# Attention step of a gated hybrid encoder: the mask and maximum of a block behind the turned copy, the variance's square a step ahead, and missing fill steps spread over the heads

## The chip, the cores and the metric

The kernel runs on one core of a Trainium2 chip. The metric is device time in microseconds (us) of the whole program, as the median of several runs. A profile is one more execution, recorded instruction by instruction. Engines: PE (TensorE, matrix products), DVE (VectorE), ACT (ScalarE), POOL (GpSimd), SP (which issues the transfers). Each works through its own instructions in order.

## The reference, cut to what matters

One layer of an encoder with two branches on the same normalised input (1024 frames of a prompt and 32 frames of a running stream, width 1024, 16 heads of 64).

```python
s = einsum('bqhd,bkhd->bhqk', q, k) + (cq - ck)      # logits with forget-gate bias
s = where(qpos >= kpos, s, lowest)                   # causal
p = softmax(s); o = einsum('bhqk,bkhd->bqhd', p, v)
conv = depthwise_conv(u_ext, w_dw) + b_dw            # 31 taps, per channel
ya = (o * silu(ga)) @ w_pa
yb = (silu(layernorm(conv)) * silu(gb)) @ w_pb       # mean and variance over 1024 channels
y  = x + (sigmoid(ma) * ya + sigmoid(mb) * yb) @ w_out
```

## The kernel before, in words

The program has three stages. First come the projections of the input for queries, keys, values, the convolution and the gate `ga`; then the attention, in which the projections of the gates `gb`, `ma` and `mb` are filled in between; then the output projections.

**The attention stage** goes over a list `seq` of 132 items: for each of 16 heads eight blocks of 128 queries (`Block`, with `i` from 0 to 7, whose keys are the first `128 * (i + 1)`), and four `Sample` items for the running stream, one after the first block of heads 3, 7, 11 and 15. In this text h2.4 is block 4 of head 2. An item passes through these methods:

- `scores` (L1110): two or four products of PE into a score tile `psS` of two banks; two such tiles rotate. In the kernel before its end also puts the causal mask on the diagonal block (L1124, DVE) and takes the negated row maximum (L1126, DVE, over all keys of the block).
- `soft` (L1129): the exponential with the maximum as bias, on ACT (L1133), into `P`.
- `norm` (L1136): the reciprocal of the row sum on DVE (L1138) and the scaling of `P` on POOL (L1139).
- `turn` (L1141): `i + 1` transposes on PE (L1153) into tiles `psT`, four to a tile, two tiles rotating. The first tile is copied out by ACT and, in blocks 4 to 7, the second by DVE (both L1156). The change's "turned copy" is this copy on DVE.
- `values` (L1158): in block 7, forty products with the values (L1172), two copies out by ACT (L1176) and DVE (L1177) and, for odd heads, the multiplication by `ga` (L1179).

The loop over `seq` (L1244) runs a software pipeline. At item `n` it calls `scores` of `n + 3`, then loads, `turn` of `n`, `soft` of `n + 3`, `norm` of `n + 2`, some fill steps, `values` of `n - 2`, as many fill steps again, and one step of the layer norm once the convolution's sums are there.

**A fill step** (`fill`, L1023) advances the generator of the gate projections by one step: three products of 352 columns (L183) and a `beat`. In all 528 such steps are to be had (22 column groups of 24 steps). They write two PSUM banks in turn, and ACT evacuates each group of eight steps (L944). Each `beat` also moves a clock that releases other work: the convolution taps on DVE (L371, one about every five beats until they are done), the loads of the next weights, their square on ACT (L117) to find a scale, and their split into a high half on ACT (L138, `wh`) and a low half on DVE (L141, `wl`).

**The layer norm's statistics** (`layernorm`, L1206) are a generator too. Its first four steps do nothing. Three steps make the mean (a product with a matrix of ones, L1202, and a scaling on ACT), three the variance, and twelve the reciprocal root. A variance step (`put`, L1213) issues the product on PE, then the square of the mean on ACT (L1215), then three DVE operations (L1216 to L1218), the first of which needs both.

**What sets the order.** In this stage the orders of PE, SP, DVE and ACT are the program's own, as the loop writes them. Only POOL's order is chosen by a scheduler. The number of fill steps around an item is written out at L1258:

```python
some = 2 if isinstance(b, Sample) or b.i > 2 or b.head.h != 8 else 0
fill(some)
...
fill(some)
```

So every item has four fill steps, and h8.0, h8.1 and h8.2 have none; with twelve steps ahead of the loop these make 528.

Of the kernel before, what the change touches and what calls it, by code (L numbers as in the profile page):

```python
# [8 lines left out]
F32 = mybir.dt.float32  # L9
# [5 lines left out]
ALU = mybir.AluOpType  # L15
AX = mybir.AxisListType

D = 1024
T = 1024
# [6 lines left out]
CH = 352  # L26
# [27 lines left out]
def build(tc, xT, xt, wv, wf, ckT, cv, clT, stT, vec, cst, yT, kT, vO, lfO, cpT, csT):  # L54
    nc = tc.nc
# [3 lines left out]
    def pool(name, bufs=1, stack=es, **kw):  # L59
        return stack.enter_context(tc.tile_pool(name=name, bufs=bufs, reuse_waits="tile", **kw))  # L60
# [19 lines left out]
    rstd = lnp.tile([128, TT], F32, name="rstd")  # L80
# [105 lines left out]
    def csl(c):  # L186
        return slice(c * CH, (c + 1) * CH)
# [88 lines left out]
    def t352(name, bufs):  # L276
        return sg.tile([128, CH], F32, name=name, tag=name, bufs=bufs)
# [5 lines left out]
    class Banks:  # L283

        n = 0
# [451 lines left out]
    for c in range(4):  # L737
# [264 lines left out]
    psT = pool("psT", 2, stack=p2, space=PS)  # L1002
# [4 lines left out]
    class Two:  # L1007
        n = 0
# [14 lines left out]
    def fill(n):  # L1023
        for _ in range(n):
            next(flow, None)

    class Sample:
# [15 lines left out]
        def scores(self):  # L1043
            g, kc, pf = self.g, self.kc, self.pf
            ps = psS.tile([128, 2, 512], F32, name="psS", tag="S")
            for j in range(4):
                rows = slice(64 * (j % 2), 64 * (j % 2) + 64)
                q = qs_t[rows, 2 * g + j // 2, :]
                nc.tensor.matmul(ps[32 * j:32 * j + 32, 0, :], q, kc[rows, j // 2, :], start=True, stop=True)
                nc.tensor.matmul(ps[32 * j:32 * j + 32, 1, :TS], q, ks_t[rows, 2 * g + j // 2, :],  # L1050
                                 start=True, stop=True)
            nc.vector.scalar_tensor_tensor(pf[:, :PAST], ps[:, 0, :], cq[:, g:g + 1], pf[:, :PAST],
                                           op0=ALU.add, op1=ALU.subtract)
# [50 lines left out]
    class Block:  # L1104
# [5 lines left out]
        def scores(self):  # L1110
            i = self.i
            QA, QB, KA, KB = self.head.q
            nk = (i + 1) * 128
            qsl = slice(i * 128, i * 128 + 128)
            ps = psS.tile([128, 2, 512], F32, name="psS", tag="S")
            nb = 1 if nk <= 512 else 2
            w = nk // nb
            wm = max(w, 256)
            for b in range(nb):
                ksl = slice(b * w, b * w + wm)  # L1120
                nc.tensor.matmul(ps[:, b, :wm], QB[:, qsl], KB[:, ksl], start=True, stop=False)  # L1121
                nc.tensor.matmul(ps[:, b, :wm], QA[:, qsl], KA[:, ksl], start=False, stop=True)  # L1122
            diag = ps[:, nb - 1, w - 128:w]
            nc.vector.tensor_add(diag, diag, cmask)  # L1124
            nm = ap.tile([128, 3], F32, name="nm", tag="nm", bufs=6)
            nc.vector.tensor_reduce(nm[:, 0:1], ps[:, :nb, :w], axis=AX.XY, op=ALU.max, negate=True)  # L1126
            self.at = ps, nm, nk, nb, w
# [55 lines left out]
    seq = []  # L1183
# [5 lines left out]
    def start(b):  # L1189
        if getattr(b, "i", 1) == 0:  # L1190
            h = b.head
            if h.h % 2 == 0:
                h.ot = heads[h.h + 1].ot = ap.tile([128, T], F32, name="ot", tag="ot", bufs=2)
        b.scores()

    def pending(b):
        return isinstance(b, Sample) or b.i % 2

    def over_channels(acc, put):
        for c in range(3):  # L1200
            pm = psT.tile([128, 512], F32, name="psn", tag="T")
            nc.tensor.matmul(pm[:, :CH], ones_f, acc[:, csl(c)], start=True, stop=True)  # L1202
            put(csl(c), pm[:, :CH])
            yield

    def layernorm():  # L1206

        shift = sides["shift"]
        for _ in range(4):
            yield  # L1210
        yield from over_channels(mean, lambda sl, ps: nc.scalar.mul(mean[:, sl], ps, 1.0 / D))

        def put(sl, ps):  # L1213
            t = t352("t", 3)
            nc.scalar.activation(t, mean[:, sl], AF.Square)  # L1215
            nc.vector.scalar_tensor_tensor(rstd[:, sl], ps, 1.0 / D, t, op0=ALU.mult, op1=ALU.subtract)  # L1216
            nc.vector.tensor_add(mean[:, sl], mean[:, sl], shift[:, sl])
            nc.vector.tensor_scalar(rstd[:, sl], rstd[:, sl], EPS, None, op0=ALU.add)  # L1218

        yield from over_channels(rstd, put)  # L1220
        for c in range(6):
            sl = slice(c * CH // 2, c * CH // 2 + CH // 2)
            v, y = rstd[:, sl], t352("t", 3)[:, :CH // 2]
            nc.scalar.activation(y, v, AF.Ln)
            nc.scalar.activation(y, y, AF.Exp, scale=-0.5)
            yield
            w = t352("t", 3)[:, :CH // 2]
            nc.vector.tensor_copy(w, v)
            newton(v, w, y)
            yield  # L1230

    ones_f = cp.tile([128, 128], F32, name="ones_f", tag="ob")
    nc.vector.memset(ones_f, 1.0)
    ln = layernorm()
    sides["shift"] = ap.tile([128, TT], F32, name="shift", bufs=1)
    nc.sync.dma_start(sides["shift"], s_m)
    heads[1].load()
    for n in range(3):
        start(seq[n])
        seq[n].soft()  # L1240
        if n:
            seq[n - 1].norm()
        fill((8, 4, 0)[n])
    for n, b in enumerate(seq):  # L1244
        if n + 3 < len(seq):
            start(seq[n + 3])
        if n + 9 < len(seq) and getattr(seq[n + 9], "i", 1) == 0:
            seq[n + 9].head.load()
        if n + 6 < len(seq) and isinstance(seq[n + 6], Sample):
            seq[n + 6].load()  # L1250
        if getattr(b, "i", 0) == 3 and b.head.h + 1 < H:
            heads[b.head.h + 1].load_v()
        b.turn()
        if n + 3 < len(seq):
            seq[n + 3].soft()
        if n + 2 < len(seq):
            seq[n + 2].norm()
        some = 2 if isinstance(b, Sample) or b.i > 2 or b.head.h != 8 else 0  # L1258
        fill(some)
        if n >= 2 and pending(seq[n - 2]):  # L1260
            seq[n - 2].values()
        fill(some)
        if n >= 3 and isinstance(seq[n - 3], Sample):
            seq[n - 3].finish()
        if "ready" in sides:
            next(ln, None)
# [17 lines left out]
    class Banks3:  # L1284
        n = 0
# [383 lines left out]
```

## Time and profile before

| | |
|---|---|
| median of 3 runs | 1348.63 us (1346.65 to 1349.82) |
| the profiled execution | 1345.89 us, of it 1344.1 us span from first to last instruction |
| attention stage in the profile | about 566 to 1053 us |
| mean granted PE clock | 0.996 |

The timeline's times are counted from the span's start. "Idle before" is the time in which an engine had nothing to run, and the name behind an arrow is what released it. Matrix products overlap one another, so their lengths may add up to more than the time they take.

### The profile page before, as it was taken

The page shows a single profiled execution, that of the slowest core. Times are in us where ns is not written, and L with a number is a line of the kernel's source. Part 1 is how long each engine was busy: PE and PEld are TensorE (multiplying, and loading weights), DVE is VectorE, ACT ScalarE, POOL GpSimd, SP SyncE. Part 2 cuts the span into 40 slices and gives each one's busy share as a digit, 9 for nine tenths or more (in the row PEclk, how much of TensorE's full clock was granted, in tenths as well). Part 3 has the DMA queues.
Part 4 walks back from the last instruction along what each step waited for, and adds up shares of the span by engine and source line. Part 5 has one row for each costly group of instructions (what it writes and reads, how often), then busy time and mean ns, then how long its engine had stood idle before and what let it go on. Part 6 is the DMA issues. An engine that isn't in the chain of part 4 may idle for free.

```text
span 1344.1 us, 24837 instructions
## 1 busy us (share of the span) xinstructions
PE 1312.6 (98%) x9383; PEld 1003.1 (75%) x9383; DVE 990.4 (74%) x1532; ACT 719.0 (53%) x1362; POOL 505.8 (38%) x548
## 2 busy tenths in 40 slices
PE   8999999999999999999889998999999999999999
PEld 5687876666666666667567766777776699999998
DVE  6797879888999997987778866655554489166664
ACT  6644555757676743455555555655555566233320
POOL 2001124547484820243433442222222158255562
PEclk8999999999999999999999999999999999999999
DMA  6343233425352463535644643565452698544462
GB/s 251 98 140 104 93 112 118 139 82 187 95 180 87 162 166 109 160 90 155 165 109 123 186 132 99 147 179 132 131 152 54 240 313 262 176 128 146 142 190 69
DMA packets 113496, 194.97 MB, mean 145 GB/s; under 512 B 34080, under 2 KB 80032, under 8 KB 113376
## 3 DMA queue, kind: packets, MB, share of 16 engines
q1 hardware_dynamic: 113232, 193.31, 46.9%
q8 instruction: 74, 1.21, 0.4%
q14 instruction: 46, 0.38, 0.1%
q10 hardware_dynamic: 144, 0.07, 0.0%
HBM read 127.68 MB, written 65.64 MB: 144 GB/s over the span
## 4 chain that ended last, share of the span: by engine, by line
PE 82%; DVE 9%; ACT 3%; issue 2%; DMA 2%; SPq 1%; POOL 0%; DVEq 0%; ACTq 0%; POOLq 0%
PE pj L183 56%; PE pjv L761 6%; PE pj L1501 6%; PE po L1172 4%; PE ptr L1153 3%; DVE nm L1126 2%; DVE wl L141 2%; DVE y L371 2%; PE psS L1122 2%; PE psS L1121 2%; DMA ga<-s_ga 2%; ACT wh L138 1%; DVE psS L1124 1%; DMA s_q<-qh 1%; PE warm L477 1%
## 5 line engine op out<-in xcount | busy, mean ns | idle before, releaser
L183 PE MATMUL pj<-xh,wh 128*128 128x352 f16 (+2 forms) x1536 | 481.6, 314 | 2.3 <-ACT wh L138 1.4
L183 PE MATMUL pj<-xh,wl 128*128 128x352 f16 (+2 forms) x1536 | 481.2, 313 | 0.7 <-DVE wl L141 0.6
L183 PE MATMUL pj<-xl,wh 128*128 128x352 f16 (+2 forms) x1536 | 480.9, 313 | 0.5 <-DVE xl L579 0.4
L183 PEld LDWEIGHTS <-wh 128*128 128x128 f16 x3072 | 301.5, 98 | 162.1 <-issue 7.1
L371 DVE SCALAR_TENSOR_TENSOR y<-u,vec_t,y 128x1086 f32<-128x1086 f32 x240 | 346.8, 1446 | 12.0 <-ACT y L368 8.9
L1139 POOL TENSOR_SCALAR P<-P,nm 128x128 f32<-128x128 f32 (+7 forms) x128 | 129.9, 1015 | 279.9 <-DVE nm L1138 229.8
L183 PEld LDWEIGHTS <-wl 128*128 128x128 f16 x1536 | 150.5, 98 | 72.0 <-DVE wl L141 1.6
L141 DVE SCALAR_TENSOR_TENSOR wl<-raw,sc,wh 128x384 f16<-128x384 f32 (+1 forms) x192 | 128.2, 693 | 48.3 <-ACT wh L138 48.3
L1133 ACT ACTIVATE P<-psS,nm 128x128 f32<-128x128 f32 (+7 forms) x128 | 95.1, 743 | 113.3 <-DVE nm L1138 70.9
L1126 DVE TENSOR_REDUCE nm<-psS 128x1 f32<-128x128 f32 (+7 forms) x128 | 97.0, 758 | 12.5
L1153 PE MATMUL ptr<-ident,P 128*128 128x128 f32 x576 | 88.6, 276 | 17.3 <-DVE pt L1156 9.2
L175 POOL TENSOR_TENSOR wl<-raw,wh 128x384 fp32r<-128x384 f32 (+1 forms) x51 | 63.3, 1270 | 74.3 <-ACT wh L172 58.6
L1153 PEld LDWEIGHTS ptr<-ident,P 128*128 128x128 f32 x576 | 69.2, 141 | 28.2 <-DVE pt L1156 12.1
L1156 ACT COPY pt<-ptr 128x512 f32<-128x512 f32 (+3 forms) x128 | 64.3, 502 | 44.4 <-PE ptr L1153 43.2
L1121 PE MATMUL psS<-KB,QB 128*128 128x256 f32 (+2 forms) x192 | 81.8, 427 | 0.6 <-ACT P L1133 0.6
L880 POOL TENSOR_TENSOR sql<-sqf,sqh 128x352 fp32r<-128x352 f32 x48 | 57.0, 1187 | 65.8 <-ACT sqh L877 65.8
L138 ACT ACTIVATE wh<-raw,sc 128x1024 f16<-128x1024 f32 (+1 forms) x68 | 73.9, 1091 | 8.2 <-DVE sc L158 7.9
L1172 PE MATMUL po<-pt,V 128*64 128x256 f32 x640 | 72.8, 382 | 2.5 <-ACT pts L1078 1.7
L1124 DVE TENSOR_TENSOR psS<-psS,cmask 128x128 f32<-128x128 f32 x128 | 37.6, 294 | 46.0 <-PE psS L1122 45.6
L906 POOL TENSOR_TENSOR ql<-qn,qh 128x352 fp32r<-128x352 f32 (+1 forms) x48 | 67.8, 1429 | 6.6 <-ACT qh L905 6.5
L761 PE MATMUL pjv<-vwh,xh 128*128 128x260 f16 x256 | 70.1, 274 | 0.0
L761 PE MATMUL pjv<-vwl,xh 128*128 128x260 f16 x256 | 70.0, 273 | 0.0
(271 smaller groups left out, 2532.9 us busy)
## 6 DMA issues: line engine op xcount, KB each, us to landing
raw<-wf SPq DMA_DIRECT2D x92, 512.0 KB
QB<-s_q SPq DMA_DIRECT2D x32, 256.0 KB
KB<-s_k SPq DMA_DIRECT2D x32, 256.0 KB
kT<-qn SPq DMA_DIRECT2D x8, 528.0 KB
s_ga<-t SPq DMA_DIRECT2D x24, 176.0 KB
s_gb<-t SPq DMA_DIRECT2D x24, 176.0 KB
s_ma<-t SPq DMA_DIRECT2D x24, 176.0 KB
s_mb<-t SPq DMA_DIRECT2D x24, 176.0 KB
```

The lines of the kernel that those rows point to most:

```text
L138: nc.scalar.mul(wh[:, ks, :], raw[:, ks, :], self.s[:, i:i + 1])
L141: nc.vector.scalar_tensor_tensor(wl[:, ks, :], raw[:, ks, :], self.s[:, i:i + 1], wh[:, ks, :], op0=ALU.mult, op1=ALU.subtract)
L183: nc.tensor.matmul(ps, a[:, kt, :], b(kt, sl), start=(first and n == 0), stop=(last and n == N - 1))
L371: t = nc.vector.scalar_tensor_tensor(y, u[:, i:i + CW], w, y, op0=ALU.mult, op1=ALU.add)
L761: nc.tensor.matmul(ps[:, :VC], a, b, start=(n == 0), stop=(n == 23))
L1121: nc.tensor.matmul(ps[:, b, :wm], QB[:, qsl], KB[:, ksl], start=True, stop=False)
L1126: nc.vector.tensor_reduce(nm[:, 0:1], ps[:, :nb, :w], axis=AX.XY, op=ALU.max, negate=True)
L1133: nc.scalar.activation(P[:, :nk].rearrange("p (b w) -> p b w", b=nb), ps[:, :nb, :w], AF.Exp, bias=nm[:, 0:1], accum_out=nm[:, 1:2])
L1139: nc.gpsimd.tensor_scalar(P[:, :nk], P[:, :nk], nm[:, 2:3], 1.0, op0=ALU.mult, op1=ALU.mult)
L1153: nc.tensor.transpose(pt[:, 128 * j:128 * j + 128], P[:, 128 * (4 * u + j):128 * (4 * u + j) + 128], ident)
L1172: nc.tensor.matmul(po[rows], V[:, j, :], parts[c][:, j, :], start=(c % 2 == 0 and j < 2), stop=(c % 2 == 1 and j >= 2 * c))
L1501: nc.tensor.matmul(pss[c][:, :HC], a[:, k, :], x, start=(not more and kt == 0 and n == 0), stop=(kt == 3 and n == 2), skip_group_check=more)
```

## The change

It has three parts.

1. The mask and the maximum leave `scores` and become a method `top` of `Block` and of `Sample`. The loop calls it after `turn` and just ahead of `soft`. On DVE the copy of block `n` now stands before mask and maximum of item `n + 3`; before it stood behind them. PE's order stays.
2. In the layer norm's variance steps the square on ACT is issued one step ahead of the product and the DVE operations that use it.
3. Head 8's three items get their four fill steps back. In heads 2 to 13 the second group of block 6 has one step instead of two. The sum is again 528.

```diff
             self.ps = ps                      # Sample
+        def top(self):
+            g, ps, pf = self.g, self.ps, self.pf
             nc.vector.scalar_tensor_tensor(pf[:, :PAST], ps[:, 0, :], ...)
...
             self.at = ps, nk, nb, w           # Block
+        def top(self):
+            ps, nk, nb, w = self.at
             diag = ps[:, nb - 1, w - 128:w]
             nc.vector.tensor_add(diag, diag, cmask)
...
-        def put(sl, ps):
+        for c in range(3):
+            sl = csl(c)
             t = t352("t", 3)
             nc.scalar.activation(t, mean[:, sl], AF.Square)
-            nc.vector.scalar_tensor_tensor(rstd[:, sl], ps, 1.0 / D, t, op0=ALU.mult, op1=ALU.subtract)
+            yield
+            pm = psT.tile([128, 512], F32, name="psn", tag="T")
+            nc.tensor.matmul(pm[:, :CH], ones_f, rstd[:, sl], start=True, stop=True)
+            nc.vector.scalar_tensor_tensor(rstd[:, sl], pm[:, :CH], 1.0 / D, t, op0=ALU.mult, op1=ALU.subtract)
             nc.vector.tensor_add(mean[:, sl], mean[:, sl], shift[:, sl])
             nc.vector.tensor_scalar(rstd[:, sl], rstd[:, sl], EPS, None, op0=ALU.add)
-
-        yield from over_channels(rstd, put)
...
         b.turn()
         if n + 3 < len(seq):
+            seq[n + 3].top()
             seq[n + 3].soft()
         if n + 2 < len(seq):
             seq[n + 2].norm()
-        some = 2 if isinstance(b, Sample) or b.i > 2 or b.head.h != 8 else 0
-        fill(some)
+        fill(2)
         if n >= 2 and pending(seq[n - 2]):
             seq[n - 2].values()
-        fill(some)
+        fill(1 if getattr(b, "i", 0) == 6 and 2 <= b.head.h < 14 else 2)
```

The first three items, ahead of the loop, call `top` right after `scores`, so their order is unchanged. The generator of the layer norm has as many steps as before; each variance product comes one step later, and the last of them in the same step as the first logarithm of the reciprocal root.

More of the change, by code (lines that the diff above doesn't have):

```diff
@@ L1051, in scores @@
                                  start=True, stop=True)
+            self.ps = ps
+        def top(self):
+            g, ps, pf = self.g, self.ps, self.pf
             nc.vector.scalar_tensor_tensor(pf[:, :PAST], ps[:, 0, :], cq[:, g:g + 1], pf[:, :PAST],
@@ L1122, in scores @@
                 nc.tensor.matmul(ps[:, b, :wm], QA[:, qsl], KA[:, ksl], start=False, stop=True)
+            self.at = ps, nk, nb, w
+        def top(self):
+            ps, nk, nb, w = self.at
             diag = ps[:, nb - 1, w - 128:w]
@@ L1239, in build @@
         start(seq[n])
+        seq[n].top()
         seq[n].soft()
```

## The prediction

> **What bounds the kernel now.** The first view is the page: which engine is busy.
>
> ```profile
> PE 1312.6 (98%) x9383; PEld 1003.1 (75%) x9383; DVE 990.4 (74%) x1532; ACT 719.0 (53%) x1362; POOL 505.8 (38%) x548
> ```
>
> TensorE (PE) is busy for all but 31.5 us of the span of 1344.1 us. The change adds and removes hardly any work, so it can win only PE's idle time, and only in the attention stage, where its lines run. The second view sums engines by stretch: attention runs from 566 to 1053 us, and I cut out 816 to 836.
>
> ```profile
> 566.00:816.00 250.00, 235.96 (x1741) 170.37 (x1739) 190.30 (x370) 140.87 (x304) 96.74 (x113) 1.00 0.49 135
> 816.00:836.00 20.00, 15.78 (x93) 10.59 (x94) 11.20 (x24) 8.72 (x18) 3.17 (x7) 0.91 0.41 104
> 836.00:1053.00 217.00, 214.13 (x1628) 155.61 (x1627) 122.67 (x305) 125.26 (x274) 54.63 (x97) 1.00 0.46 128
> ```
>
> After the stretch and its length stand the busy times of PE, weight load, DVE, ACT and POOL, then PE's clock. PE idles 14.0, 4.2 and 2.9 us: 21.1 us in all, a fifth of it in the 20 us of head 8, and there the clock falls to 0.91. The groups by line say what ends this idle time (last columns).
>
> ```profile
> L1153 PE MATMUL ptr<-ident,P 128*128 128x128 f32 x576 | 88.6, 276 | 17.3 <-DVE pt L1156 9.2 <-ACT pt L1156 6.4 <-DVE ot L1177 1.2
> L1172 PE MATMUL po<-pt,V 128*64 128x256 f32 x640 | 72.8, 382 | 2.5 <-ACT pts L1078 1.7 <-ACT mean L1211 0.7
> ```
>
> So 17.3 of 21.1 us stand in front of the transposes, which wait until one of the two psT tiles has been copied out: 9.2 us for the DVE copy, 6.4 us for the ACT copy. The DVE copy exists only in blocks 4 to 7 of a head. I write h2.4 for head 2, block 4.
>
> **Part 1: mask and maximum behind the copy, gain.** Here is a DVE that runs late (h2.4, the maximum is that of h2.7), from the timeline: start, length, engine, line, and in brackets the idle time before and its releaser.
>
> ```profile
> 648.02 0.29 DVE L1124 TENSOR_TENSOR psS<-psS,cmask 128x128 f32<-128x128 f32 x1
> 648.41 1.22 DVE L1126 TENSOR_REDUCE nm<-psS 128x1 f32<-128x1024 f32 x1
> 649.55 0.28 DVE L1156 COPY pt<-ptr 128x128 f32<-128x128 f32 x1
> 649.75 1.12 ACT L1133 ACTIVATE P<-psS,nm 128x1024 f32<-128x1024 f32 x1 [1.79 <-DVE nm L1126]
> 649.89 0.44 PE L1153 MATMUL ptr<-ident,P 128*128 128x128 f32 x2 [1.16 <-DVE pt L1156]
> ```
>
> The copy starts 1.53 us after the mask. Put first, it starts at 648.02 and PE's 1.16 us are gone. The price is that the exponential of the new block starts later by the copy's 0.28 us. No instruction and no DMA is added: scores, mask, maximum and copy are the same ones. The other waits of this kind:
>
> ```profile
> 592.04 0.55 PE L1153 MATMUL ptr<-ident,P 128*128 128x128 f32 x3 [1.74 <-DVE pt L1156]
> 595.82 0.66 PE L1153 MATMUL ptr<-ident,P 128*128 128x128 f32 x4 [0.65 <-DVE pt L1156]
> 684.78 0.44 PE L1153 MATMUL ptr<-ident,P 128*128 128x128 f32 x2 [0.61 <-DVE pt L1156]
> 688.18 0.55 PE L1153 MATMUL ptr<-ident,P 128*128 128x128 f32 x3 [0.49 <-DVE pt L1156]
> 692.57 0.66 PE L1153 MATMUL ptr<-ident,P 128*128 128x128 f32 x4 [1.27 <-DVE pt L1156]
> 770.10 0.44 PE L1153 MATMUL ptr<-ident,P 128*128 128x128 f32 x2 [0.83 <-DVE pt L1156]
> 777.79 0.66 PE L1153 MATMUL ptr<-ident,P 128*128 128x128 f32 x4 [1.01 <-DVE pt L1156]
> ```
>
> Those at 649.89, 770.10 and 777.79 stand alone and I take them whole: 1.16 + 0.83 + 1.01 = 3.0 us. The two runs (592.04 and 595.82; 684.78 to 692.57) are different: DVE is busy with convolution taps and weight splits from one wait to the next, so what is late next is DVE's own queue. A copy moved ahead of a short mask and maximum comes about 0.3 + 0.4 us earlier, and that is won once per run, not per wait: I take 0.65 us each, 1.3 us of 4.76. The remaining 9.2 - 7.76 = 1.4 us lie after 816 us; of them I take half, 0.7. Term A: -5.0 us, bounds 0 and -9.2.
>
> **Part 1, price.** When PE sets the pace, DVE comes to the mask before the transposes are done. Then the copy at the head of DVE's queue makes it idle. What is queued behind: mask, maximum, reciprocal; behind the maximum waits ACT with the exponential, and behind that in ACT's order the weight split, a gate's evacuation and the next block's ACT copy, for which PE waits. The timeline at h12.4 and h12.5:
>
> ```profile
> 948.66 0.71 PE L1153 MATMUL ptr<-ident,P 128*128 128x128 f32 x5
> 948.86 0.30 DVE L1124 TENSOR_TENSOR psS<-psS,cmask 128x128 f32<-128x128 f32 x1 [0.92 <-PE psS L1122]
> 950.40 0.28 DVE L1156 COPY pt<-ptr 128x128 f32<-128x128 f32 x1
> 950.92 1.02 POOL L1139 TENSOR_SCALAR P<-P,nm 128x896 f32<-128x896 f32 x1 [1.92 <-DVE nm L1138]
> 951.71 1.14 ACT L138 ACTIVATE wh<-raw,sc 128x1024 f16<-128x1024 f32 x1
> 953.18 0.58 ACT L1156 COPY pt<-ptr 128x512 f32<-128x512 f32 x1
> 953.92 0.61 PE L1153 MATMUL ptr<-ident,P 128*128 128x128 f32 x4
> 955.01 0.55 PE L1153 MATMUL ptr<-ident,P 128*128 128x128 f32 x3 [0.47 <-DVE pt L1156]
> ```
>
> The transposes end at 949.37. With some 0.08 us for the signal the copy runs 949.45 to 949.73, and the mask starts at 949.73 and not at 948.86: the exponential is 0.87 us later. ACT's copy of h12.5, which ends at 953.76, would end that much later, and the transposes that need its tile start at 953.92: a slack of 0.16, so a new wait of 0.71 us. Normalising on POOL, which also moves by up to 0.87, keeps its cover: it ends at 951.94 for transposes that start at 953.92. The same subtraction elsewhere:
>
> ```profile
> 619.57 0.58 ACT L1156 COPY pt<-ptr 128x512 f32<-128x512 f32 x1
> 620.30 0.38 PE L1153 MATMUL ptr<-ident,P 128*128 128x128 f32 x2
> 981.10 0.58 ACT L1156 COPY pt<-ptr 128x512 f32<-128x512 f32 x1
> 981.84 0.38 PE L1153 MATMUL ptr<-ident,P 128*128 128x128 f32 x2
> ```
>
> These are h1.5 and h13.5, with slacks of 0.15 and 0.16. A split (1.14 us) or its square stands ahead of the copy in all three; where none does, the slack is longer by about that. Term B: three hops of 0.71, +2.1 us; bounds 0 and, at every hop of 14 heads, 9.9.
>
> **Part 2 and 3: head 8.** Before, blocks h8.0 to h8.2 issue no fill steps, just when the variance products run. Twelve steps come back there.
>
> ```profile
> 816.20 4.54 PE L1172 MATMUL po<-pt,V 128*64 128x256 f32 x40 [0.65 <-ACT mean L1211]
> 823.48 0.52 PE L1153 MATMUL ptr<-ident,P 128*128 128x128 f32 x3 [1.25 <-DVE ot L1177]
> 824.57 0.86 PE L1202 MATMUL psn<-rstd,ones_f 128*128 128x352 f32 x2 [0.57 <-ACT pt L1156]
> 828.08 0.53 DVE L1216 SCALAR_TENSOR_TENSOR rstd<-psn,t 128x352 f32<-128x352 f32 x1 [1.44 <-ACT t L1215]
> 834.27 0.33 PE L1153 MATMUL ptr<-ident,P 128*128 128x128 f32 x1 [2.20 <-ACT pt L1156]
> 834.60 1.49 PE pj L183 x10
> ```
>
> PE idles 0.65 + 1.25 + 0.57 + 2.20 = 4.67 us. A fill step is three products at 0.149 us (ten take 1.49 in the chain of waits, last row), 0.45 us; twelve bring 5.4 us of PE work to where the waits are, so DVE and ACT catch up behind it. The square a step earlier takes away the 1.44 us that DVE spent waiting for it ahead of mask and maximum. Then the clock, by windows:
>
> ```profile
> 822.10:825.51 3.41, 1.59 (x8) 1.03 (x8) 3.31 (x7) 0.48 (x1) 0.00 (x0) 1.00 0.19 73
> 825.51:828.92 3.41, 3.41 (x14) 2.38 (x13) 1.87 (x4) 1.85 (x4) 0.80 (x1) 0.50 0.66 157
> ```
>
> After a window with 1.59 us of PE work the clock is half for 3.41 us, with PE busy throughout: 1.7 us lost. At stake are 6.4 us. [...] I leave 1.9 us of waits: one variance step of DVE (0.52 + 0.51 + 0.33 us) in front of a copy, and one ACT operation of 0.5. Term C: -4.5, bounds 0 and -6.4.
>
> The twelve steps are taken from block 6 of heads 2 to 13, 0.45 us of cover each. Stores of gates and weight loads on SP's queue move with the beats by at most twelve steps; they have several blocks' lead, and I cost them at nothing. What hides the lost cover is the slack of ACT's copy of block 6 against the transposes of block 7:
>
> ```profile
> 982.48 0.58 ACT L1156 COPY pt<-ptr 128x512 f32<-128x512 f32 x1 [0.44 <-PE ptr L1153]
> 984.74 0.71 PE L1153 MATMUL ptr<-ident,P 128*128 128x128 f32 x5
> ```
>
> This is 1.68 us; the later exponential of block 5's step takes up to 1.1, the fill 0.45, and about 0.1 is left. So it holds unless a split of 1.14 us falls there. I take three heads of twelve at 0.45. Term D: +1.4, bounds 0 and +5.4.
>
> **The sum:** -5.0 + 2.1 - 4.5 + 1.4 = -6.0 us. The profiled execution took 1345.9 us (its span 1344.1); after would be 1339.9. The runs shown have a median of 1348.6, 2.7 us above it; the forecast in their terms is 1342.6 us.
>
> **Rivals.** *Everything goes* (A at 9.2, C at 6.4, half of ACT's other waits hidden by the added cover, B and D near 2): about -13 us, 1335.6. Against it speaks that in the two runs DVE itself is late.
>
> *The waits only move*: A is cancelled by B and D near the middle of their bounds, C brings 1 to 2 us because the variance's 1.4 us of DVE work per block now meets h8.4 to h8.6 with their large maxima: -1 us, 1347.6. For it speaks that a longer queue on DVE shows again at its next hand-over.
>
> *Slower: DVE blocked behind transposes.* The mechanism is that of B: the copy waits for PE, and the exponential waits behind it. It decides from some thirteen hops of 0.71 us on, since A and C bring 9.5. If the fill drift puts splits or squares ahead of the copy in all 14 heads that PE paces: 14 x 0.71 = 9.9, all of D 5.4, less 9.5: +5.8, 1354.4. [...] Against it: 0.16 us of slack is the exception, found with a split or square ahead.
>
> **Chances.** Forecast (gain of 3 to 9 us) 0.58; everything goes 0.10; only moved 0.17; slower 0.15. A measurement of this kernel can tell about 0.2%, 2.7 us, from no change. Faster 0.68, same 0.17, slower 0.15. The range 1335.5 to 1351.5 takes in the first three and leaves out most of the last.
>
> **What would show it.** After the change, transposes' idle time ended by the DVE copy should fall from 9.2 to some 4 us, that ended by the ACT copy (4.2 of 6.4 lie outside 834.27) should grow by 1 to 3, the exponential's wait for the maximum on ACT should grow, and the half clock near 825 us should be gone. If ACT-copy waits in blocks 5 and 6 sum to over 9 us, the slower rival was right; if the DVE-copy waits stay near 9 us, DVE's load and not its order was the bound.

## The result, and the profile after

Over 14 runs of each, the kernel after took 1344.02 us in the median (1342.07 to 1346.47) and the kernel before 1348.77 us (1345.03 to 1354.26): a ratio of 0.996, 95% interval 0.9949 to 0.9972, so a gain of 3.8 to 6.9 us. The forecast gain of 6.0 us lies in this interval, and the forecast 1342.6 us is 1.4 us below the measured median. The profiled execution took 1344.6 us (span 1342.8). That is only 1.3 us less than the profiled execution before, so the two profiles show where waits went, but not the whole gain. The first line of the one after, engine by engine:

```profile
PE 1313.1 (98%) x9383; PEld 1001.9 (75%) x9383; DVE 987.7 (74%) x1532; ACT 715.5 (53%) x1362; POOL 512.1 (38%) x548
```

PE has the same work and idles 29.7 us where it idled 31.5. The attention stage by stretches, with the columns as before (busy times of PE, weight load, DVE, ACT, POOL, then PE's clock):

```profile
566.00:816.00 250.00, 234.91 (x1725) 168.09 (x1723) 186.67 (x364) 136.99 (x297) 100.44 (x112) 1.00 0.49 133
816.00:836.00 20.00, 20.00 (x138) 14.14 (x135) 13.36 (x28) 10.80 (x24) 4.33 (x8) 1.00 0.51 132
836.00:1053.00 217.00, 214.10 (x1620) 154.80 (x1619) 123.67 (x310) 124.82 (x276) 56.00 (x97) 1.00 0.47 128
```

Head 8 (second row) is full: PE idles nothing of 20 us, and the clock there is 1.00 where it was 0.91. The stretch ahead of it is no better: 15.1 us idle against 14.0. The groups by line say what became of it, first the scores' line of before, then three lines of after:

```profile
L1121 PE MATMUL psS<-KB,QB 128*128 128x256 f32 (+2 forms) x192 | 81.8, 427 | 0.6 <-ACT P L1133 0.6
```

```profile
L1161 PE MATMUL ptr<-ident,P 128*128 128x128 f32 x576 | 88.3, 275 | 12.6 <-ACT pt L1164 5.9 <-DVE pt L1164 3.4 <-POOL P L1147 2.4
L1125 PE MATMUL psS<-KB,QB 128*128 128x256 f32 (+2 forms) x192 | 81.5, 426 | 2.6 <-ACT P L1141 2.6
L1180 PE MATMUL po<-pt,V 128*64 128x256 f32 x640 | 73.0, 382 | 2.3 <-ACT pts L1082 2.2
```

(L1125, L1161, L1164, L1147, L1141, L1146 and L1180 are the lines that were L1121, L1153, L1156, L1139, L1133, L1138 and L1172.) The transposes wait 3.4 us for the DVE copy, not 9.2. But ACT's copy still costs 5.9 although head 8 no longer has any of it, POOL's scaling costs 2.4, and the scores wait 2.6 us for the exponential, before 0.6. That the chain behind the copy got later shows on the waits of the other engines (time, count, the longest). Before:

```profile
ACT P L1133 <- DVE nm L1138: 70.9, 62, 3.1
ACT P L1133 <- DVE nm L1126: 38.4, 30, 3.3
DVE pt L1156 <- PE ptr L1153: 1.4, 2, 1.2
```

And after:

```profile
ACT P L1141 <- DVE nm L1146: 134.8, 102, 3.7
DVE pt L1164 <- PE ptr L1161: 34.5, 27, 2.7
```

DVE now stands 34.5 us ahead of its copy, waiting for transposes, and ACT's waiting for the maximum grew from 109.3 (70.9 + 38.4) to 134.8 us. (Where the short reciprocal, L1138 or L1146, follows the maximum on DVE, the view names it; by the program the exponential needs the maximum alone, so all three rows are read as waits for the maximum.) That is the mechanism of the rival "slower", at work in 27 places.

One thing no single profile shows: the kernel before spreads over 9 us from run to run, the kernel after over 4 (in e5 below, the same kernel run again, over 7.6). Much of this goes with each run's mean granted PE clock. Over 74 runs of the kernel before, on three chips:

| mean granted clock of the run | 0.991 | 0.992 | 0.993 | 0.994 | 0.995 | 0.996 |
|---|---|---|---|---|---|---|
| runs | 4 | 14 | 4 | 23 | 22 | 7 |
| mean time, us | 1353.3 | 1352.6 | 1351.7 | 1350.9 | 1348.8 | 1347.4 |

That is -1.23 us per 0.001 of clock (correlation -0.81; in proportion it would be 1.35). The profile of before that I read was one of the better runs (0.996). The average run has 0.994, and each of the 14 runs after has 0.996 or more. So below I split each result in two: the mean of time times clock, which is about the time at full clock and changes with **waits**, and the mean clock. The split is an estimate: the slope is 1.23 and not 1.35, and some of the clock's spread has nothing to do with the attention stage. Of half-clock windows the 14 profiles have one to three in their first 30 us (three in e6, one in e11), where all these kernels do the same.

### The profile page after: what moved, and what is told of

Read it like the earlier page. It is cut to its first block, busy times and chain, and to the rows that moved or that the text cites. A ratio compares the mean times of both kernels' runs of the same rounds, so it can differ in the third digit from the quotient of the medians.

```text
span 1342.8 us, 24833 instructions
## 1 busy us (share of the span) xinstructions
PE 1313.1 (98%) x9383; PEld 1001.9 (75%) x9383; DVE 987.7 (74%) x1532; ACT 715.5 (53%) x1362; POOL 512.1 (38%) x548
## 4 chain that ended last, share of the span: by engine, by line
PE 79%; DVE 9%; DMA 3%; ACT 3%; issue 3%; SPq 1%; POOL 1%; DVEq 0%; POOLq 0%; ACTq 0%
PE pj L183 55%; PE pjv L761 6%; PE pj L1512 6%; PE po L1180 4%; PE ptr L1161 3%; DMA ga<-s_ga 2%; DVE y L371 2%; DVE nm L1134 2%; PE psS L1125 2%; PE psS L1126 1%; DVE wl L141 1%; ACT wh L138 1%; DVE pt L1164 1%; ACT P L1141 1%; DVE psS L1132 1%
## 5 line engine op out<-in xcount | busy, mean ns | idle before, releaser
L1147 POOL TENSOR_SCALAR P<-P,nm 128x128 f32<-128x128 f32 (+7 forms) x128 | 135.2, 1056 | 264.9 <-DVE nm L1146 233.9
L1141 ACT ACTIVATE P<-psS,nm 128x128 f32<-128x128 f32 (+7 forms) x128 | 95.0, 742 | 138.7 <-DVE nm L1146 134.8
L1161 PE MATMUL ptr<-ident,P 128*128 128x128 f32 x576 | 88.3, 275 | 12.6 <-ACT pt L1164 5.9
L1161 PEld LDWEIGHTS ptr<-ident,P 128*128 128x128 f32 x576 | 68.6, 141 | 24.8 <-POOL P L1147 7.0
L1125 PE MATMUL psS<-KB,QB 128*128 128x256 f32 (+2 forms) x192 | 81.5, 426 | 2.6 <-ACT P L1141 2.6
L1164 ACT COPY pt<-ptr 128x512 f32<-128x512 f32 (+3 forms) x128 | 64.2, 502 | 32.4 <-PE ptr L1161 32.3
L138 ACT ACTIVATE wh<-raw,sc 128x1024 f16<-128x1024 f32 (+1 forms) x68 | 73.9, 1091 | 8.1 <-DVE sc L158 7.9
L1180 PE MATMUL po<-pt,V 128*64 128x256 f32 x640 | 73.0, 382 | 2.3 <-ACT pts L1082 2.2
L120 POOL CAST topb<-tops 128x2 bf16<-128x2 f32 x35 | 19.4, 555 | 136.5 <-ACT junk L117 86.6
L761 PE MATMUL pjv<-vwh,xl 128*128 128x260 f16 x256 | 69.9, 273 | 0.0
```

The source lines that it names most:

```text
L138: nc.scalar.mul(wh[:, ks, :], raw[:, ks, :], self.s[:, i:i + 1])
L761: nc.tensor.matmul(ps[:, :VC], a, b, start=(n == 0), stop=(n == 23))
L1141: nc.scalar.activation(P[:, :nk].rearrange("p (b w) -> p b w", b=nb), ps[:, :nb, :w], AF.Exp, bias=nm[:, 0:1], accum_out=nm[:, 1:2])
L1147: nc.gpsimd.tensor_scalar(P[:, :nk], P[:, :nk], nm[:, 2:3], 1.0, op0=ALU.mult, op1=ALU.mult)
L1161: nc.tensor.transpose(pt[:, 128 * j:128 * j + 128], P[:, 128 * (4 * u + j):128 * (4 * u + j) + 128], ident)
L1180: nc.tensor.matmul(po[rows], V[:, j, :], parts[c][:, j, :], start=(c % 2 == 0 and j < 2), stop=(c % 2 == 1 and j >= 2 * c))
```

## The experiments

My theory was the forecast's: the waits for DVE's copy go (part 1), head 8's waits and half clock go (parts 2 and 3), and a small price is paid. The rival: part 1 only moves waits, and the gain is head 8's. After the first runs a second question came up: how much is clock. Each kernel ran beside the kernel before on the same chip (median of before 1351.08 us for e1 to e4, 1350.13 for e5 to e8, 1350.23 for e9 to e12). "Waits" is the change of mean time times clock against before, in us, with a standard error of 0.4 to 0.6; the clock is a mean over runs of a value given to 0.001.

| kernel | median us | ratio, 95% interval | waits | clock, before |
|---|---|---|---|---|
| e1 part 1 alone | 1353.51 | 1.0016 (1.0005 to 1.0027) | +3.0 | 0.9941, 0.9937 |
| e2 part 3 alone | 1348.75 | 0.9983 (0.9969 to 0.9997) | -0.7 | 0.9950, 0.9937 |
| e3 parts 2 and 3 | 1346.42 | 0.9961 (0.9947 to 0.9975) | -3.8 | 0.9944, 0.9937 |
| e4 whole, scaling first | 1348.71 | 0.9981 (0.9971 to 0.9992) | +1.5 | 0.9967, 0.9937 |
| e5 whole again | 1345.48 | 0.9971 (0.9957 to 0.9985) | -0.4 | 0.9967, 0.9940 |
| e6 whole, fewer taps | 1345.36 | 0.9964 (0.9951 to 0.9978) | -1.8 | 0.9962, 0.9940 |
| e7 whole, some behind | 1345.01 | 0.9966 (0.9952 to 0.9980) | -2.3 | 0.9955, 0.9940 |
| e8 whole, step from block 1 | 1344.17 | 0.9958 (0.9944 to 0.9971) | -1.6 | 0.9970, 0.9940 |
| e9 parts 2 and 3, block 1 | 1346.37 | 0.9973 (0.9960 to 0.9986) | -1.8 | 0.9955, 0.9940 |
| e10 e9 with spread steps | 1346.37 | 0.9976 (0.9962 to 0.9990) | -0.7 | 0.9959, 0.9940 |
| e11 whole with spread steps | 1349.41 | 0.9994 (0.9985 to 1.0004) | +3.1 | 0.9967, 0.9940 |
| e12 e7 with spread steps | 1348.99 | 0.9991 (0.9979 to 1.0003) | +1.1 | 0.9958, 0.9940 |

### e1_top_only: part 1 alone

```diff
         b.turn()
         if n + 3 < len(seq):
+            seq[n + 3].top()
             seq[n + 3].soft()
```

(with `top` taken out of `scores` as in the change; the rest as before)

> Part 1 alone (mask and maximum behind the turned copy), fill steps and variance as before. Theory A (the prediction's): the order on DVE pays by itself; waits of transposes for the DVE copy fall from 9.3 to some 4 us, waits elsewhere grow by 2 to 3, the attention stage goes from 486.8 us to about 483 to 484 and the time by -3 us. Theory B (formed from the profile after the change, where PE's waits for POOL, for the exponential and for the ACT copy grew by about as much as those for the DVE copy fell): the new waits eat the gain; stage 485.5 to 488, time within 1.5 us of before, the half clock near head 8 still there.

Part 1 alone makes the kernel slower, by 0.7 to 3.6 us; theory A expected a gain of 3 us, theory B a difference of at most 1.5. The transposes' group by line, and the place in head 8 where the trace of before showed 2.20 us (timeline):

```profile
L1161 PE MATMUL ptr<-ident,P 128*128 128x128 f32 x576 | 88.6, 277 | 18.9 <-ACT pt L1164 9.7 <-DVE pt L1164 6.7 <-DVE ot L1185 1.5
```

```profile
839.10 1.01 ACT L1141 ACTIVATE P<-psS,nm 128x896 f32<-128x896 f32 x1 [2.26 <-DVE nm L1146]
...
840.10 1.14 ACT L138 ACTIVATE wh<-raw,sc 128x1024 f16<-128x1024 f32 x1
841.14 0.54 ACT L944 ACTIVATE t<-pj,sc 128x352 f32<-128x352 f32 x1
...
841.58 0.49 ACT L1223 ACTIVATE t<-mean 128x352 f32<-128x352 f32 x1
...
841.96 0.58 ACT L1164 COPY pt<-ptr 128x512 f32<-128x512 f32 x1
...
842.59 0.47 PE L1161 MATMUL ptr<-ident,P 128*128 128x128 f32 x1 [3.48 <-ACT pt L1164]
```

The DVE copy's 9.2 became 6.7 and ACT's 6.4 became 9.7. The timeline shows how: an exponential that starts late pushes the split (L138), a gate's evacuation, the variance's square and only then the copy, all in ACT's order, and PE waits 3.48 us, longer than before. DVE's copies give back 2.5 us, ACT's take 3.3, and the products with the values wait 5.3 us where they waited 2.5. The forecast's net of A and B (-2.9) has the wrong sign for part 1 by itself. The profile overstates the loss: it is of one of the slowest of the 12 runs (1355.56 us), and 3.51 of the DVE copy's 6.7 us are one wait at 652 us that the last section traces to chance. With 1.35 us there, as in the kernel after, it would be 4.5, about what the forecast expected.

### e2_fills_only and e3_fills_square: part 3 alone, parts 2 and 3

```diff
-        some = 2 if isinstance(b, Sample) or b.i > 2 or b.head.h != 8 else 0
-        fill(some)
+        fill(2)
...
-        fill(some)
+        fill(1 if getattr(b, "i", 0) == 6 and 2 <= b.head.h < 14 else 2)
```

This is e2; e3 has the variance loop of the change as well. Mask and maximum stay ahead of the copy in both.

> Part 3 alone (fill steps given back to head 8 and taken from block 6 of heads 2 to 13). Theory A: 4.7 us of waits and 1.7 us of half clock at head 8, less 1.9 that stay, less 1.4 for the cover lost in block 6: -3 us, stage about 484. Theory B: the fill steps carry nearly the whole change: -4 to -6 us, stage 481 to 483, no half clock inside the stage.

> Parts 2 and 3 (fill steps and the square a step ahead), mask and maximum ahead of the copy as before. Theory A: as the fill steps alone, and up to 1.4 us less, slower than the whole change by about 3 us. Theory B: level with the whole change or faster than it (-5 to -7 us against before), since part 1 nets nothing.

Fills alone bring 0.4 to 4.2 us, and with the square moved 3.4 to 7.2: parts 2 and 3 reach by themselves a ratio that can't be told from the whole change's. The profile of e2 still has four half-clock windows in the stage, where its theory B expected none. What part 2 does shows in the timelines. First e2, two steps of the variance:

```profile
837.51 1.01 ACT L1133 ACTIVATE P<-psS,nm 128x896 f32<-128x896 f32 x1 [2.49 <-DVE nm L1138]
...
838.51 0.48 ACT L1215 ACTIVATE t<-mean 128x352 f32<-128x352 f32 x1
...
839.03 0.52 DVE L1216 SCALAR_TENSOR_TENSOR rstd<-psn,t 128x352 f32<-128x352 f32 x1 [1.16 <-ACT t L1215]
...
839.53 0.33 PE L1153 MATMUL ptr<-ident,P 128*128 128x128 f32 x1 [1.62 <-ACT pt L1156]
...
844.45 0.44 PE L1153 MATMUL ptr<-ident,P 128*128 128x128 f32 x2 [1.54 <-ACT pt L1156]
```

And e3:

```profile
832.27 1.01 ACT L1133 ACTIVATE P<-psS,nm 128x896 f32<-128x896 f32 x1 [1.37 <-DVE nm L1138]
...
833.27 0.49 ACT L1216 ACTIVATE t<-mean 128x352 f32<-128x352 f32 x1
...
833.65 0.58 ACT L1156 COPY pt<-ptr 128x512 f32<-128x512 f32 x1
```

In both kernels the square stands ahead of ACT's copy, so that is not what differs. In e2 the exponential starts late, after 2.49 us of waiting, because the three DVE operations of the variance step before stand ahead of the mask; behind it the copy is late, and PE waits 1.62 us. DVE then waits 1.16 us for the square with the next mask behind it, and one step later PE waits 1.54 us. In e3 the variance step comes one item later and its square is ready: DVE waits for no square, the exponential waits 1.37 us, and PE's two waits are gone, 3.2 us. The two kernels differ by as much in waits (-3.8 against -0.7), but that is partly luck: PE's idle time as a whole differs by 1.7 us between these two profiles, because other waits differ too.

### e4_norm_first: POOL's scaling ahead of mask and maximum

```diff
         if n + 3 < len(seq):
+            if n + 2 < len(seq):
+                seq[n + 2].norm()
             seq[n + 3].top()
             seq[n + 3].soft()
```

> The whole change, and the reciprocal of item n+2 (DVE) moved ahead of mask and maximum of item n+3, so that POOL can scale P earlier by mask and maximum (0.7 to 1.6 us). Theory B: the 2.4 us of waits of transposes for POOL's scaling come from the reciprocal standing behind a later maximum; they go, and the time falls 2 to 3 us below that of the whole change. Rival: DVE and ACT are late there in any case, and the wait goes over to the ACT copy (exponential 0.15 us later): within 1 us of the whole change.

This was to take away the new 2.4 us in front of the transposes. The reciprocal of the block n + 2 then stands ahead of the mask of n + 3. The transposes by line:

```profile
L1161 PE MATMUL ptr<-ident,P 128*128 128x128 f32 x576 | 88.6, 276 | 13.4 <-ACT pt L1164 8.3 <-DVE pt L1164 2.2 <-DVE nm L1069 1.1
```

POOL's wait has left the list, ACT's copy went from 5.9 to 8.3, and the scores' wait for the exponential from 2.6 to 3.7. The reciprocal needs the previous exponential's sum, so mask and maximum now wait on DVE for it and the next exponential is later still. In the trace DVE waits 18.5 us for it in 23 places (0.7 in the whole change). The wait moved on to who stands behind it, as the rival said, and the kernel came out at 0.9981, where the whole change had 0.9960 and, in e5, 0.9971: more of a loss than the 1 us of the rival.

### e5_whole_again, e6_taps_slower, e7_some_behind: the whole change, and two lighter ones

e5 is the whole change unaltered, beside the next two on one chip. e6 issues fewer convolution taps per beat of the attention stage; e7 puts `top` behind the copy only for block 4 and where item n + 3 is a `Sample`:

```diff
-R_U, R_V, R_QK, R_G, R_A = 0.21, 0.18, 0.165, 0.23, 0.2
+R_U, R_V, R_QK, R_G, R_A = 0.21, 0.18, 0.165, 0.23, 0.165
```

```diff
+        behind = n + 3 < len(seq) and (getattr(b, "i", 0) == 4 or isinstance(seq[n + 3], Sample))
+        if n + 3 < len(seq) and not behind:
+            seq[n + 3].top()
         b.turn()
-        if n + 3 < len(seq):
+        if behind:
             seq[n + 3].top()
```

> The whole change again, beside the others of this call on one chip. Theory C (formed from the first four runs): PE's clock is half for a window of 3.41 us after any such window in which PE was busy for less than about half of it; the kernel before loses some 5 us a run that way inside the attention stage, two or three windows, and the whole change loses none, so most of its gain is clock and not waits. Expected: ratio 0.994 to 0.998 against before, mean granted clock 0.997 in nearly every run against 0.991 to 0.996 of before, spread of the runs half as wide. If the gain were waits alone, clocks would be alike.

> The whole change with the convolution taps spread thinner over the fill steps (0.165 a beat in place of 0.2), so that DVE has 18% less of them in each block of heads 0 to 7 and they last into head 9 or 10. Theory C with DVE's load as the cause of the waits: waits of transposes between 585 and 790 us (about 11 us after the change) fall to 6 to 8, time 2 to 4 us below the whole change. Rival: those waits come from the order of ACT and DVE at single blocks (splits ahead of copies), not from the load: within 1.5 us of the whole change.

> The whole change, but mask and maximum go behind the turned copy only where they are long: in block 4 of a head (maximum over 1024 keys) and where item n+3 is a Sample; elsewhere they stand ahead of turn, as before. Theory A: block 4 and the Samples hold 3.0 to 3.6 us of the 5.8 us by which waits for the DVE copy fell, and the later exponential of blocks 5 to 7 is spared, so waits for POOL (2.4) and for the exponential (2.7) shrink by about half: 1 to 2 us below the whole change. Theory C: the waits left in blocks 5 to 7 of heads 2 and 3 fall together in single windows again; half-clock windows come back in some runs (mean clock 0.995 to 0.996) and the time is 1 to 3 us above the whole change.

The three are within each other's intervals. e5's ratio and clock came out as expected, its spread did not: 7.6 us against before's 6.8 on that chip. e5 splits the whole change's gain: its mean is 4.0 us below before's, of which 0.4 is waits and 3.6 is clock (0.9967 against 0.9940). Against e3 the waits are worse by 3.4 us and the clock better by about 0.002; on two chips, the ratios 0.9961 and 0.9971 can't be told apart. So, on top of parts 2 and 3, part 1 seems to lose in waits what it brings in clock. e7 lies between the two in waits and in clock, as a half change would; neither of its theories' times can be told from the whole change's. In e6 the transposes' waits between 585 and 790 us are 6.2 us, where the kernel after has 9.8, as the theory of DVE's load had it. But between 825 and 910 us PE waits 5.5 us, where the kernel after has 1.5, and the time did not fall by the 2 to 4 us that it asked for.

### e8_step_from_block1 and e9_ahead_block1: where the missing step is taken from

```diff
-        fill(1 if getattr(b, "i", 0) == 6 and 2 <= b.head.h < 14 else 2)
+        fill(1 if getattr(b, "i", 0) == 1 and 2 <= b.head.h < 14 else 2)
```

e8 is the whole change with this line, e9 parts 2 and 3 with it, so that they differ by part 1 alone.

> The whole change, but the step that heads 2 to 13 give up is taken from block 1 (behind the 4.5 us of value products) in place of block 6. Theory A, term D: the lost cover in block 6 costs 1.4 us, seen as waits of about 0.7 us each for the ACT copy near 720 and 812 us that the kernel before does not have; they go: 1 to 2 us below the whole change. Rival: they come from where the splits fall, and the shift only moves them: within 1 us.

> Parts 2 and 3 with the missing step taken from block 1 (as the best of the last four), but mask and maximum ahead of the copy, as before the change. It differs from that best one by part 1 alone. Theory C (part 1 brings clock, not waits): mean granted clock 0.994 to 0.996 against 0.997 with part 1, and the time with the clock's loss taken off (time multiplied by clock) no more than with part 1; 0 to 3 us slower than with part 1. Theory A (part 1 brings waits): 3 us slower at the same clock.

The whole change shows two waits of the kind that term D foresaw, in block 7 behind ACT's copy (timeline):

```profile
720.69 0.66 PE L1161 MATMUL ptr<-ident,P 128*128 128x128 f32 x4 [0.73 <-ACT pt L1164]
...
812.11 0.66 PE L1161 MATMUL ptr<-ident,P 128*128 128x128 f32 x4 [0.82 <-ACT pt L1164]
```

With block 6's step given back, in e8, they stay:

```profile
719.29 0.66 PE L1161 MATMUL ptr<-ident,P 128*128 128x128 f32 x4 [0.68 <-ACT pt L1164]
...
810.49 0.66 PE L1161 MATMUL ptr<-ident,P 128*128 128x128 f32 x4 [0.68 <-ACT pt L1164]
```

So the lost cover of block 6 did not make them; my theory missed here and its rival held. They came with part 3: e2, e3 and e9, which leave mask and maximum ahead of the copy, have both (0.68 us each), and e1, which lacks part 3, has neither. e2 to e9 all have one fill step, and so one beat, less in each of heads 2 to 13, whichever block gives it up; that the shifted beats make these waits is argued, not shown. e8's ratio of 0.9958 is the lowest of all, but not to be told from the whole change's. e8 against e9 repeats one half of the balance above: the clock is 0.9970 with part 1 and 0.9955 without, as the clock theory (theory C) expected, but the waits are -1.6 and -1.8. Here part 1 brings clock and costs no waits that show. So whether it costs waits on top of parts 2 and 3 stays open, and how it brings clock was not shown.

### e10_ahead_spread, e11_behind_spread, e12_some_spread: cover put where the waits are

From the places where PE still waits (heads 0, 2 and 3) I chose six blocks that get a third step in the second group, and took them from blocks where the trace had no wait:

```diff
+    EXTRA = {(0, 4), (0, 5), (2, 2), (2, 3), (2, 4), (3, 4)}
...
+        if (h, i) in EXTRA:
+            return 3
+        return 1 if (i == 1 and 4 <= h < 16) or (i == 2 and 9 <= h < 15) else 2
...
-        fill(1 if getattr(b, "i", 0) == 6 and 2 <= b.head.h < 14 else 2)
+        fill(steps_after(b))
```

e10 is e9 with this, e11 the whole change, e12 e7.

> As the one before (mask and maximum ahead of the copy), with one more fill step behind the blocks where transposes wait in a cluster (h0.4, h0.5, h2.2, h2.3, h2.4, h3.4), six steps taken from block 2 of heads 9 to 14, where PE waits for nothing. The same products are done in all. Theory C: the windows in which PE is busy for less than half vanish with the added work, so the clock rises to 0.996 or 0.997 and the time falls by 2 to 4 us against the one before. Rival: each added step brings a fifth of a tap (0.27 us) to DVE, which is what is late there, and the waits stay: within 1 us.

> The whole change with fill steps spread as in the run before. Its clock is 0.997 already, so theory C expects from the added cover only waits: 0 to 2 us below the whole change, clock unchanged.

> Mask and maximum behind the copy only in block 4 and for Samples, fill steps spread as in the two runs before. If waits and clock add up as theory C has it: waits as with that order (some 2 us fewer than the whole change, by time multiplied by clock) and a clock of 0.996 to 0.997: 1342 to 1344 us against some 1350 before, the fastest of all. If the split beside POOL's addition near 650 us (2.56 us in place of 0.47) still falls into a wait there, one window stays at half clock and it is level with the whole change.

Theory C missed in all three: e10 gained nothing over e9, as its rival had it, and e11 and e12 lost 3 to 4 us against the kernels without it. In e11's profile the transposes' waits grew from 12.6 to 13.7 us and the products with the values wait 5.0 us where they waited 2.3:

```profile
L1161 PE MATMUL ptr<-ident,P 128*128 128x128 f32 x576 | 88.0, 275 | 13.7 <-ACT pt L1164 6.7 <-DVE pt L1164 2.8 <-POOL P L1147 1.9
L1180 PE MATMUL po<-pt,V 128*64 128x256 f32 x640 | 73.5, 382 | 5.0 <-DVE ot L1185 2.9 <-ACT pt L1164 1.4 <-ACT pts L1082 0.8
```

A fill step is also a beat, so moving one shifts every tap, split and evacuation behind it against the blocks; a new wait for DVE's copy of the output (2.9 us) came with that. All three kernels of this group have it (near 759 and 942 us), and no other kernel. Which shifted operation made it was not tried and stays open. e4 and e11 also show that the clock does not simply follow the waits: both have more of them than the kernel before, and a clock of 0.9967. No kernel of this study clearly beats the whole change.

## Why the prediction was right in its sum, and where its steps were not

**Term A (-5.0).** Right in its sum, a little small: the transposes' waits for the DVE copy fell from 9.2 to 3.4 us, -5.8. By places it was luck. Of the three waits that I took whole, 3.0 us, only the 0.83 at 770.10 is gone. The 1.01 at 777.79 became the wait for POOL shown below, 0.97. At 649.89, my lead example, PE waits 1.35 us in the kernel after, in place of 1.00 for ACT's copy and 1.16 for DVE's:

```profile
650.96 0.84 PE L1161 MATMUL ptr<-ident,P 128*128 128x128 f32 x6 [1.35 <-DVE pt L1164]
```

The copy is first now, but a tap and a split of 1.04 us stand ahead of it on DVE. The run of 684.78 to 692.57, from which I took 0.65 of 2.37 us, shrank to 0.37 for the DVE copy.

**Term B (+2.1): the step that failed.** The mechanism was right (ACT's waits for the maximum grew by 25.5 us), its size and place were not. POOL's 2.4 (before 0.5 at most), the scores' 2.0, and ACT's copy outside head 8, from 4.2 to 5.9, make about 6, of which 1.55 are term D's two waits below; that leaves about 4.4, twice the forecast. (The 0.08 us for the signal in its hops was an estimate of mine: in the trace of before, the copies of ACT and DVE that wait for transposes start 0.04 us after them.) So A, B and D together are nothing, as "the waits only move" had it, and not -1.5. The place: I looked for short slack at h1.5, h12.5 and h13.5, where PE sets the pace. The waits came mostly in heads 0 to 7, where taps and splits load DVE as well. And "normalising on POOL keeps its cover" was read from h12.4, where the scaling took 1.02 us. By form, scaling 896 and 1024 elements in heads 0 to 7 and then, from 836 us on, in the kernel before:

```profile
L1139 POOL TENSOR_SCALAR P<-P,nm 128x896 f32<-128x896 f32 x8 | 12.2, 1531 | 18.3 <-DVE nm L1138 16.5 <-PE pj L183 1.7
L1139 POOL TENSOR_SCALAR P<-P,nm 128x1024 f32<-128x1024 f32 x8 | 12.0, 1502 | 8.2 <-ACT P L1133 4.5 <-DVE nm L1138 3.5
```

```profile
L1139 POOL TENSOR_SCALAR P<-P,nm 128x1024 f32<-128x1024 f32 x8 | 9.1, 1133 | 6.5 <-DVE nm L1138 6.4
L1139 POOL TENSOR_SCALAR P<-P,nm 128x896 f32<-128x896 f32 x8 | 8.7, 1085 | 23.4 <-DVE nm L1138 20.5 <-DVE sc L157 2.9
```

The trace of before held it: the scaling of a large block takes 1.5 us in the heads with taps and 1.1 without. In the timeline after, one of them is late and long, and PE waits:

```profile
776.10 0.47 DVE L141 SCALAR_TENSOR_TENSOR wl<-raw,sc,wh 128x256 f16<-128x256 f32 x1
...
776.36 2.38 POOL L1147 TENSOR_SCALAR P<-P,nm 128x1024 f32<-128x1024 f32 x1 [0.50 <-DVE nm L1146]
...
776.49 1.34 DVE L371 SCALAR_TENSOR_TENSOR y<-u,vec_t,y 128x1086 f32<-128x1086 f32 x1
...
778.79 0.98 PE L1161 MATMUL ptr<-ident,P 128*128 128x128 f32 x7 [0.97 <-POOL P L1147]
```

**Term C (-4.5).** Right, and too careful: head 8 gave all 4.67 us of waits and the 1.7 of half clock in the profile, -6.4; no 1.9 were left. It takes parts 2 and 3 both: e2 keeps 1.62 and 1.54 us of waits that e3 has lost.

**Term D (+1.4).** Two waits of 0.73 and 0.82 us stand there, 1.55 in all. The size was right by luck: they came with part 3, but not from the lost cover of block 6, as e8 shows.

**What the sum left out.** I counted one half-clock window because the one profile had one. The average run of the kernel before loses 0.003 of clock more than the run after, about 4 us, which at 1.7 us a window is two to three of them. In e5 this is nearly all of the gain. That these windows lie in the attention stage was not measured for the runs without a profile; it is argued from the other stages being the same in both kernels. Waits that I took to cancel within B and D did cost, and clock that I had not counted paid for it: the total was right partly because two errors met. Idle rows also flatter: from first scores to last value product the profile's stage shrank by 2.6 us, while idle fell by 3.1 (21.1 to 18.0 in the rows by stretch) and half clock by 1.7. The rest is pauses that the modelled ends of the previous products hide (a fill product's row is 0.31 us long, though they start 0.149 us apart): between a fill product and the scores behind it +1.4 us, between scores and transposes +0.9.

**The rivals.** "Slower" was right in direction for part 1 alone (2.4 us by the medians, not 5.8) and lost only to parts 2 and 3. "Everything goes" was refuted by the waits that took the place of the DVE copy's.

## What to carry to other kernels

DVE and ACT ran their instructions in the program's order here: in the kernel before, the mask at 829.20 us stood behind DVE's wait of 1.44 us although its scores had ended at 826.73. So a wait removed by the swap went to whoever stood behind the swapped instruction (transposes' waits for DVE's copy fell by 5.8 us, those behind it grew by about 4.4); price that chain in the most loaded part of the stage, not where its rows are easiest to read. Where runs of one kernel spread, put time against granted clock before explaining a few us: time times clock separates waits from clock. A cluster of short waits cost as much again by the half clock behind it in e6 (next section: 1.6 us of idle time, then 1.7 us of lost clock), so a change may pay by spreading waits that it does not remove. And before a wait in one profile is put down to a change, see whether the instructions up to it differ at all.

## What the runs showed of the hardware

**The clock fell after full-clock windows in which PE was busy for 53% or less.** Half clock came in windows of 3.41 us. Here are two windows with the one that follows, from e3 and e6 (after the length stands PE's busy time; the clock is ahead of the last two numbers):

```profile
648.16:651.57 3.41, 0.44 (x4) 0.20 (x2) 3.31 (x3) 0.00 (x0) 2.07 (x2) 1.00 1.00 213
651.57:654.99 3.42, 3.06 (x11) 1.79 (x12) 2.52 (x8) 3.20 (x7) 2.63 (x2) 0.50 0.26 66
```

```profile
828.20:831.61 3.41, 1.79 (x11) 1.25 (x11) 2.99 (x8) 1.57 (x3) 0.97 (x1) 1.00 0.68 185
831.61:835.02 3.41, 3.41 (x15) 2.13 (x13) 2.94 (x7) 2.38 (x7) 1.90 (x2) 0.50 0.00 0
```

PE was busy for 13% and 52% of the window, and each time the next ran at half clock. In the attention stages of all 14 profiles, 14 windows at full clock were followed by half clock, with PE busy for under 1% (e1, from 839.10 us) to 53%; none above 53% was. Below 47% all were but one (44%, in the kernel before from 832 us). Between 47% and 53% three of 17 were; in e5, 48% did no harm:

```profile
663.10:666.51 3.41, 1.64 (x15) 0.91 (x14) 2.85 (x6) 2.75 (x7) 1.87 (x3) 1.00 0.92 237
666.51:669.92 3.41, 3.41 (x34) 2.27 (x32) 0.68 (x1) 1.38 (x4) 0.89 (x4) 1.00 1.07 231
```

Twice, in e1 and e2 near 650 us, a half-clock window was followed by a second one although PE was busy for 78% and 73% of it; why stays open. The runs show these shares and not what sets the clock. Whether a cluster of waits fills half of a window would depend on where the window begins, which would help to explain why runs of one kernel differ; that is argued, not shown.

**Side by side, an instruction of DVE or of POOL took longer.** In e3 the last split of a weight stood beside POOL's additions of the convolution:

```profile
645.42 1.10 POOL L1139 TENSOR_SCALAR P<-P,nm 128x768 f32<-128x768 f32 x1 [4.81 <-DVE nm L1138]
...
645.66 1.99 DVE L371 SCALAR_TENSOR_TENSOR y<-u,vec_t,y 128x1086 f32<-128x1086 f32 x1
...
647.43 2.80 POOL L351 TENSOR_TENSOR rstd<-rstd,y 128x1024 f32<-128x1024 f32 x2 [0.92 <-ACT y L355]
647.57 2.56 DVE L141 SCALAR_TENSOR_TENSOR wl<-raw,sc,wh 128x256 f16<-128x256 f32 x1
...
651.92 0.69 PE L1153 MATMUL ptr<-ident,P 128*128 128x128 f32 x2 [3.33 <-DVE pt L1156]
```

In the kernel before the split came ahead of the additions:

```profile
645.55 2.28 POOL L1139 TENSOR_SCALAR P<-P,nm 128x768 f32<-128x768 f32 x1 [4.81 <-DVE nm L1138]
...
645.79 1.35 DVE L371 SCALAR_TENSOR_TENSOR y<-u,vec_t,y 128x1086 f32<-128x1086 f32 x1
...
647.05 1.04 DVE L141 SCALAR_TENSOR_TENSOR wl<-raw,sc,wh 128x256 f16<-128x256 f32 x1
...
647.80 3.75 POOL L351 TENSOR_TENSOR rstd<-rstd,y 128x1024 f32<-128x1024 f32 x2
```

The same split of 256 columns took 2.56 us, until POOL's additions were nearly done. It took 1.04 us in the kernel before, where POOL's scaling ran until 647.83 beside it, and 0.47 us at 776.10 in the kernel after (above). In e3 PE then waited 3.33 us for the copy, and the clock halved: that is the window of e3 above. e1 and e7 have the same wait at the same place, 3.51 and 3.52 us.

Scaling and tap ran side by side both times, and one of them was drawn out: in e3 the tap (1.99 us, before 1.35), in the kernel before the scaling (2.28 us, in e3 1.10). Which of the two it will be can't be read from the rows: POOL's starts 0.24 us ahead of the tap's in both. Why one of them lengthens was not shown.

**The same order gives either outcome.** Up to 655 us e3 and the kernel before run the same instructions in the same order on PE, DVE, ACT and POOL (the first fill step that part 3 takes away is in h2.6). Still the scaling and the tap went one way in e3 and the other way before, and PE's wait near 650 us was 3.33 us and 1.16. e1 and the kernel after are alike in the same way up to 657 us, with 3.51 and 1.35 us. So this difference belongs to the single execution and not to a change, and it is one source of the spread between runs of one kernel. How often each outcome comes was not measured.
